# A two-layer hybrid trunk on one NeuronCore: the convolution's first tap on ScalarE into PSUM, wider channel statistics, and the last weight splits placed between taps

## The chip, the core and the metric

The kernel runs on one core of one Trainium2 chip. The metric is the device time of one execution in microseconds; 522.5 us is the median of three runs before the change. The profiled execution is a run of its own, at 522.39 us.

## What is computed

The input x is 512 tokens by 1024 channels in fp32. Layer 0 is attention (two groups of heads, a gate and an output projection). The change lies in layer 1, whose reference, cut to what matters, is

```
val, glu_gate, z = split(rms_norm(x) @ w_in, 3)          # 1024 -> 3 x 1024
u = val * sigmoid(glu_gate)
u = causal depthwise conv(u, conv_w, width 31) + conv_b   # per channel, over tokens
u = silu(layer_norm(u)) * silu(z)                         # layer norm over channels
return x + u @ w_out
```

## The kernel before, in words

Every weight matrix comes in chunks of 256 columns. `fetch` loads a chunk from memory into one of two staging buffers `wst` (L148, on SP's queue); `split_w` (L155) then makes two tensors from it: `hi`, the weight rounded to TensorE's fp32r type, and `lo`, the rest. For most late chunks both come from transfers that POOL issues: a casting transfer `hi<-wst` (L169), and, after ScalarE has written the negated rounded weight into `lo` (L175, or L160 for chunk 32), an accumulating transfer that adds `wst` to it (L179, L161). `ahead(n)` (L807) splits chunks up to n-1 and, behind each, asks for the next chunk's load. That load has to wait until the accumulating transfer out of the same staging buffer has landed. Each product is three matmuls: hi by hi, hi by lo, lo by hi.

In layer 1 the channels are eight tiles of 128. For a tile, TensorE makes value and gate (`glu`, L733), ScalarE a tanh, and VectorE the product `u` (L745, one of three buffers). The 31 taps of the convolution are shared out (`conv_steps`, L748): VectorE adds 15 to 21 of them into `acc`, a PSUM bank (tags `s`, two banks); the first goes into an SBUF tile `first` with the bias added (L763), the second reads `first` and writes `acc`, the rest run in place (L766). ScalarE multiplies the others into `tm` (L775, six buffers; the first of them straight into `pacc`, L772), and POOL adds each `tm` to the SBUF sum `pacc` (L776, two buffers). A tile ends when VectorE adds `acc` and `pacc` (L783, the final sum). `conv_out` (L793) then has TensorE transpose the tile back to tokens (L796), VectorE take statistics of each 128 tokens by 128 channels out of PSUM (L798), and ScalarE copy it to `ctok` (L799).

Tiles 0 and 1 are worked in two halves of 256 tokens, tiles 2 to 5 whole, and tiles 6 and 7, the late ones, in two halves again. Up to L968 the compiler's scheduler sets the order on each engine, by a simulated timeline and program order as priority: the first halves of tiles 6 and 7 (written 6a and 7a here; 18 additions on POOL), and between them `z_chunk` for chunks 28 to 30 with `ahead(34)`, `ahead(35)` and `ahead(36)`, which split chunks 33, 34 and 35 (L966 to L968).

From L1013 the order on TensorE, VectorE, ScalarE and POOL is written out by hand. `na()` emits the next few ScalarE-and-POOL taps of 6b and 7b, the second halves, by the list `AQ` (4, 0, 7, 1, 0, 1, 2, ...), and `nd()` the next few VectorE taps by `DQ` (3, 5, 2, 0, 0, ...). The stretch opens with

```
conv_out(6); z matmuls of tile 6; na(): 4 taps; nd(): 3 taps
conv_out(7); na(): none; z_act(6); norm_stats(0)
z matmuls of tile 7, 6 of 8 steps; na(): 7 taps; nd(): 5 taps
norm_cols(0, 0); ng_t(0, 0); ng_t(0, 1); the other 2 steps of tile 7; norm_cols(0, 1)
```

where `norm_stats` (L900) is two aggregates and an addition on VectorE and a power on POOL (L905), `norm_cols` (L907) normalises `ctok` on VectorE (L911), and `ng_t` transposes it on TensorE (L922). The 5 taps of the second `nd()` are, in this order, 6b's fourth, 7b's first, 6b's fifth, 7b's second, 6b's sixth. Four phases p = 0 to 3 follow for the first half of the tokens: per phase two silus (L928), taps, products with z (L933), rounding (L936), the rest (L939), and 24 output matmuls (L361). Chunks 33 and 34 are used in them, 32 and 35 behind them, beside the second half's `conv_out` and norm.

## Time and profile before

| what | value |
|---|---|
| median of 3 runs (lowest to highest) | 522.5 us (522.39 to 523.61) |
| the profiled execution's own time | 522.39 us |
| its span, first to last instruction | 520.6 us |
| TensorE matmul busy | 503.7 us, 97% of the span |
| VectorE, ScalarE, POOL busy | 373.0, 329.1, 232.6 us |

Times in the rows are microseconds from the span's start unless marked ns. PE is TensorE, PEld its weight loads, DVE VectorE, ACT ScalarE, POOL GpSimd; SP issues plain loads and stores. A row of the order of instructions gives start, duration, engine, line, operation, output<-inputs, shape and count; the square bracket is the engine's idle time just before it and what ended it. TensorE's rows overlap, as its matmuls are pipelined.

### The profile page before, as it was taken

The numbers are of one execution on the slowest core, as the hardware profiler recorded it, in microseconds if no ns is written. First come the engines' busy times: TensorE is split into PE (matmuls) and PEld (weight loads), VectorE is DVE, ScalarE is ACT, GpSimd is POOL, SyncE is SP. The second block draws the span as 40 slices with busy tenths as digits, with TensorE's granted clock in tenths as the row PEclk, the third lists the DMA queues.
The fourth block names the chain that finished last, engine by engine and source line by source line (L and its number), as shares of the span: only waits on it lengthen the run. The fifth ranks groups of instructions, "written<-read, shape, count | busy, mean of one in ns | idle before, by whom it ended". The sixth has DMA issues, their size and how long they took to land.

```text
span 520.6 us, 9754 instructions
## 1 busy us (share of the span) xinstructions
PE 503.7 (97%) x3694; PEld 459.9 (88%) x3694; DVE 373.0 (72%) x788; ACT 329.1 (63%) x668; POOL 232.6 (45%) x255
## 2 busy tenths in 40 slices
PE   8999999999999999999999999999999999769997
PEld 4999998987889988788789999999999888548997
DVE  7745677676465577596685256999999997868741
ACT  4945678777645775576384735998676765377230
POOL 5264852020422233223101113879988985687200
PEclk9999999999999999999999999999999999989999
DMA  8742222302122242402219668488999799962111
GB/s 293 318 145 81 84 81 83 102 24 83 61 102 94 82 111 99 144 14 108 102 52 395 130 205 242 82 211 286 235 306 259 212 270 305 262 170 105 41 51 42
DMA packets 16566, 79.05 MB, mean 152 GB/s; under 512 B 1988, under 2 KB 4352, under 8 KB 8712
## 3 DMA queue, kind: packets, MB, share of 16 engines
q1 hardware_dynamic: 12632, 51.08, 27.1%
q0 software_dynamic: 3744, 27.26, 22.0%
q8 instruction: 29, 0.48, 0.4%
q10 hardware_dynamic: 144, 0.09, 0.1%
q14 instruction: 17, 0.14, 0.1%
HBM read 50.07 MB, written 2.14 MB: 100 GB/s over the span
## 4 chain that ended last, share of the span: by engine, by line
PE 70%; DMA 8%; POOL 7%; ACT 6%; DVE 4%; issue 3%; SPq 0%; POOLq 0%; ACTq 0%
PE mm L361 29%; POOL pacc L776 6%; PE mm L370 6%; PE mm L371 6%; PE mm L372 6%; DMA wst<-in_w_dram 5%; PE st L361 4%; PE o L603 3%; PE tp L526 3%; PE o L361 2%; PE s L510 2%; PE s L512 2%; DMA wlo<-wst 1%; DMA xt<-in_xt_dram 1%; PE s L361 1%
## 5 line engine op out<-in xcount | busy, mean ns | idle before, releaser
L776 POOL TENSOR_TENSOR pacc<-pacc,tm 128x256 f32<-128x256 f32 (+1 forms) x125 | 120.7, 986 | 15.8 <-ACT tm L775 10.1
L766 DVE SCALAR_TENSOR_TENSOR s<-u,parts,s 128x256 f32<-128x256 f32 (+1 forms) x211 | 108.1, 569 | 0.5
L361 PE MATMUL mm<-wlo,hhi 128*128 128x256 f32 (+1 forms) x352 | 98.7, 287 | 0.8 <-DVE wlo L177 0.5
L361 PE MATMUL mm<-whi,hhi 128*128 128x256 f32 (+1 forms) x352 | 98.4, 287 | 0.0
L361 PE MATMUL mm<-whi,hlo 128*128 128x256 f32 (+1 forms) x352 | 98.3, 286 | 0.0
L775 ACT ACTIVATE tm<-u,parts 128x256 f32<-128x256 f32 (+1 forms) x125 | 66.2, 571 | 14.5 <-POOL pacc L776 14.0
L361 PEld LDWEIGHTS mm<-wlo,hhi 128*128 128x128 f32 x352 | 65.8, 190 | 2.0 <-DVE wlo L177 0.8
L361 PEld LDWEIGHTS mm<-whi,hhi 128*128 128x128 f32 x352 | 65.6, 189 | 0.7 <-issue 0.2
L361 PEld LDWEIGHTS mm<-whi,hlo 128*128 128x128 f32 x352 | 65.9, 190 | 0.2
L177 POOL TENSOR_TENSOR wlo<-wst,whi 128x512 fp32r<-128x512 f32 (+1 forms) x22 | 31.0, 1423 | 57.4 <-ACT whi L173 57.4
L173 ACT ACTIVATE whi<-wst 128x512 fp32r<-128x512 f32 (+2 forms) x77 | 49.4, 707 | 5.9 <-DMA wst<-in_w_dram 2.7
L518 POOL TENSOR_TENSOR cb<-cb,mask 128x128 f32<-128x128 f32 x32 | 15.5, 490 | 80.7 <-DVE nm L522 46.2
L523 ACT ACTIVATE p<-p,nm 128x128 f32<-128x128 f32 (+3 forms) x64 | 35.7, 559 | 24.1 <-DVE nm L522 23.6
L177 DVE TENSOR_TENSOR wlo<-wst,whi 128x512 fp32r<-128x512 f32 (+1 forms) x50 | 39.8, 830 | 9.0 <-PE o L361 7.1
L370 PE MATMUL mm<-nhi,wx 128*128 128x256 f32 (+1 forms) x104 | 33.0, 318 | 0.0
L371 PE MATMUL mm<-nlo,wx 128*128 128x256 f32 (+1 forms) x104 | 32.2, 309 | 0.0
L372 PE MATMUL mm<-nhi,wx 128*128 128x256 f32 (+1 forms) x104 | 31.9, 307 | 0.0
L371 PE MATMUL mm<-nlo,whi 128*128 128x256 f32 (+1 forms) x104 | 31.8, 307 | 0.0
L372 PE MATMUL mm<-nhi,wlo 128*128 128x256 f32 (+1 forms) x104 | 31.7, 306 | 0.0
L370 PE MATMUL mm<-nhi,whi 128*128 128x256 f32 (+1 forms) x104 | 31.7, 307 | 0.0
L526 PE MATMUL tp<-identf,p 128*128 128x128 f32 x160 | 28.4, 275 | 1.1 <-ACT p L523 0.7
L396 POOL TENSOR_TENSOR rq<-vq,mhalf 128x16 f32<-128x16 f32 x8 | 26.2, 3272 | 6.2 <-DVE vq L394 6.1
(292 smaller groups left out, 1436.3 us busy)
## 6 DMA issues: line engine op xcount, KB each, us to landing
wst<-in_w_dram SPq DMA_DIRECT2D x33, 1024.0 KB, 5.0
wx<-wst POOLq DMA_DIRECT2D x13, 1024.0 KB, 7.2
wlo<-wst POOLq DMA_DIRECT2D x8, 1024.0 KB, 8.4
whi<-wst POOLq DMA_DIRECT2D x3, 1024.0 KB, 4.5
wst<-in_w_dram SPq DMA_DIRECT2D x2, 1040.0 KB
xs<-in_x_dram SPq DMA_DIRECT2D x4, 512.0 KB, 10.3
cb<-cdram SPq DMA_DIRECT2D x8, 256.0 KB, 3.5
x<-in_x_dram SPq DMA_DIRECT2D x4, 512.0 KB, 6.5
```

The source lines that it names most:

```text
L173: A.activation(hi[:, ks], st[:, ks], AF.Copy)
L177: (V if eng is G and parts == 4 and k % 4 and V0 else eng).tensor_tensor(lo[:, ks], st[:, ks], hi[:, ks].bitcast(F32), op=ALU.subtract)
L361: T.matmul(po, a[:, k, ts], b[:, k, :n], start=first and i == 0, stop=last and i == len(prods) - 1)
L370: T.matmul(po, whi[:, k, cs], a, start=k == 0, stop=False)
L371: T.matmul(po, whi[:, k, cs], b, start=False, stop=False)
L372: T.matmul(po, wlo[:, k, cs], a, start=False, stop=k == KC - 1)
L396: G.tensor_tensor(r, v, mhalf[:, :16].rearrange("p (t h) -> p t h", t=NT), op=ALU.pow)
L523: A.activation(p[:, :w], p[:, :w], AF.Exp, bias=nm, scale=-1.0, accum_out=sm[:, h, t:t + 1])
L526: T.transpose(tp[:, j * P:(j + 1) * P], p[:, j * P:(j + 1) * P], identf)
L766: V.scalar_tensor_tensor(acc[:, o], v, w, first[0][:, :n] if i == 1 else acc[:, o], op0=ALU.mult, op1=ALU.add)
L775: A.activation(tm[:, :n], v, AF.Copy, scale=w)
L776: G.tensor_tensor(pacc[:, o], pacc[:, o], tm[:, :n], op=ALU.add)
```

## The change

The first VectorE tap of a tile becomes a ScalarE activation that writes the PSUM accumulator directly. Statistics of tiles 0 to 3 and of tiles 4 and 5 are taken from `ctok` in SBUF, 512 and 256 channels wide, once the last of them is copied; tiles 6 and 7 keep theirs from PSUM. `pacc` gets a third buffer. The casting transfers of chunks 22, 26, 27, 28, 30, 31, 33, 34 and 35 read the weights in memory and not the staging buffer. The splits of chunks 33 and 34 are ordered behind the ScalarE and the POOL instruction of the 9th and the 17th of the 20 taps of 6a and 7a; the split of chunk 35 moves to the end of phase p = 1. The silu results take pairs out of the buffers of tag `sg`.

```diff
     def split_w(w, ring, eng, parts, cast):
-        st, n = w
+        (st, n), src = w
...
         if cast:
-            G.dma_start(hi, st)
+            G.dma_start(hi.rearrange("p k n -> p (k n)"), w_ap(*src, 0, KC))
...
-    stats = l1.tile([P, NT, KC, 6], F32, name="stats")
+    stats = l1.tile([P, NT, 4, 6], F32, name="stats")
...
             if i == 0:
-                first.append(l1.tile([P, S], F32, tag="first", name="first", bufs=FB))
-                V.tensor_scalar(first[0][:, :n], v, w, cbias[:, ct:ct + 1], op0=ALU.mult,
-                                op1=ALU.add)
+                A.activation(acc[:, o], v, AF.Identity, bias=cbias[:, ct:ct + 1], scale=w)
             else:
-                V.scalar_tensor_tensor(acc[:, o], v, w, first[0][:, :n] if i == 1 else acc[:, o],
-                                       op0=ALU.mult, op1=ALU.add)
+                V.scalar_tensor_tensor(acc[:, o], v, w, acc[:, o], op0=ALU.mult, op1=ALU.add)
...
-        for t in range(t0, t0 + n):
-            V.bn_stats(stats[:, t, ct, :], pt[:, t * P:(t + 1) * P])
+        if ct >= KC - NLATE:
+            for t in range(t0, t0 + n):
+                V.bn_stats(stats[:, t, ct - 4, :], pt[:, t * P:(t + 1) * P])
         A.activation(ctok[:, t0:t0 + n, ct * P:(ct + 1) * P],
                      pt[:, t0 * P:(t0 + n) * P].rearrange("p (t c) -> p t c", t=n), AF.Copy)
+        if ct in (3, 5):
+            for t in range(t0, t0 + n):
+                V.bn_stats(stats[:, t, ct // 5, :], ctok[:, t, 4 * (ct // 5) * P:(ct + 1) * P])
...
-        return l1.tile([P, S], F32, tag="pacc", name="pacc", bufs=2)
+        return l1.tile([P, S], F32, tag="pacc", name="pacc", bufs=3)
...
-        c = cs_[h, k] = l1.tile([P, HT], F32, tag="c", name="c", bufs=CB)
+        if k % 2 == 0:
+            cp[0] = l1.tile([P, 2, HT], F32, tag="sg", name="c", bufs=2)
+        c = cs_[h, k] = cp[0][:, k % 2]
...
+    taps = []
     for i in range(max(len(a6), len(a7) + LAGA)):
         j = i - LAGA
         for f in a6[i:i + 1] + (a7[j:j + 1] if j >= 0 else []):
-            f()
+            taps.append(f())
...
     for c in range(3):
         z_chunk(28 + c, c)
-        ahead(34 + c)
+        if c < 2:
+            with tc.issue_after(taps[TW[c]][0].ins), tc.issue_after(taps[TW[c]][1].ins):
+                ahead(34 + c)
...
             for (c, t), po in zip(units, banks):
                 out1_mm(c, t, po, (2 * p, 2 * p + 1))
+            if p == 1:
+                ahead(36)
```

`TW` is (8, 16), `CB` was 3.

## Rows read from the trace of the kernel before

**Rows 1.** The page's first part: busy time of each engine, its share of the span, and its instructions.

```profile
PE 503.7 (97%) x3694; PEld 459.9 (88%) x3694; DVE 373.0 (72%) x788; ACT 329.1 (63%) x668; POOL 232.6 (45%) x255
```

**Rows 2.** Busy time by stretch: the stretch, its length, then each engine's busy time (instructions), the granted TensorE clock, the DMA share and GB/s.

```profile
320.00:442.50 122.50, 122.07 (x902) 115.43 (x900) 118.72 (x238) 94.00 (x142) 102.64 (x107) 1.00 0.86 239
...
461.20:465.00 3.80, 3.73 (x13) 3.13 (x13) 3.74 (x7) 1.42 (x3) 3.48 (x5) 0.55 0.93 185
478.00:517.80 39.80, 39.25 (x327) 38.48 (x325) 20.78 (x53) 9.89 (x22) 6.85 (x10) 1.00 0.15 51
```

**Rows 3.** The order of TensorE's instructions from 442 us.

```profile
444.35 0.44 PE L796 MATMUL tp<-identf,pacc 128*128 128x128 f32 x2 [1.48 <-DVE pacc L783]
...
452.04 0.41 PE L796 MATMUL tp<-identf,pacc 128*128 128x128 f32 x2 [1.74 <-DVE pacc L783]
...
460.50 0.30 PE L922 MATMUL tp<-identf,ctok 128*128 128x128 f32 x1 [3.92 <-DVE ctok L911]
461.27 1.68 PE L922 MATMUL tp<-identf,ctok 128*128 128x128 f32 x7 [0.47 <-DVE ctok L911]
...
465.53 0.38 PE L361 MATMUL st<-whi,u 128*128 128x256 f32 x1 [0.28 <-ACT u L936]
```

**Rows 4.** The order of VectorE's instructions from 443 us.

```profile
443.87 0.42 DVE L783 TENSOR_TENSOR pacc<-s,pacc 128x256 f32<-128x256 f32 x1 [3.68 <-POOL pacc L776]
...
451.46 0.42 DVE L783 TENSOR_TENSOR pacc<-s,pacc 128x256 f32<-128x256 f32 x1
452.49 0.49 DVE L798 BATCH_NORM_STATS2 stats<-tp 128x6 f32<-128x128 f32 x2 [0.60 <-PE tp L796]
...
453.52 0.17 DVE L904 TENSOR_SCALAR lnv<-mv 128x2 f32<-128x2 f32 x1
...
459.40 3.55 DVE L911 TENSOR_SCALAR ctok<-ctok,mv,lnr 128x512 f32<-128x512 f32 x4 [3.82 <-POOL lnr L905]
```

**Rows 5.** The order of POOL's instructions, the late ones; DMA_DIRECT2D is the issue of a transfer.

```profile
421.08 9.50 POOL L776 TENSOR_TENSOR pacc<-pacc,tm 128x512 f32<-128x512 f32 x9
434.93 0.60 POOL L169 DMA_DIRECT2D whi<-wst  x1 [4.34 <-DMA wst<-in_w_dram]
...
442.43 9.13 POOL L776 TENSOR_TENSOR pacc<-pacc,tm 128x256 f32<-128x256 f32 x12 [0.20 <-ACT pacc L772]
456.02 0.60 POOL L169 DMA_DIRECT2D wx<-wst  x1 [4.47 <-DMA wst<-in_w_dram]
...
458.36 1.01 POOL L905 TENSOR_TENSOR lnr<-lnv,mhalf 128x2 f32<-128x2 f32 x1
```

**Rows 6.** The additions of L776 alone, by stretch: the stretch, its length, POOL's busy time with them (how many), the granted TensorE clock, the DMA share and GB/s.

```profile
430.60:451.60 21.00, 12.04 (x16) 1.00 1.00 298
```

**Rows 7.** The order of ScalarE's instructions from 434 us.

```profile
434.47 1.92 ACT L175 ACTIVATE wlo<-wst 128x2048 fp32r<-128x2048 f32 x1 [5.29 <-DMA wst<-in_w_dram]
...
455.53 1.91 ACT L175 ACTIVATE wx<-wst 128x2048 fp32r<-128x2048 f32 x1 [6.85 <-DMA wst<-in_w_dram]
457.35 0.37 ACT L799 ACTIVATE ctok<-tp 128x256 f32<-128x256 f32 x1
...
458.09 2.89 ACT L775 ACTIVATE tm<-u,parts 128x256 f32<-128x256 f32 x7
```

**Rows 8.** Groups of instructions by line and shape, from 315 us to the end: count, busy us, mean ns of one, and idle time before them.

```profile
L766 DVE SCALAR_TENSOR_TENSOR s<-u,parts,s 128x256 f32<-128x256 f32 x139 | 60.7, 479 | 0.5
L766 DVE SCALAR_TENSOR_TENSOR s<-u,parts,s 128x512 f32<-128x512 f32 x72 | 50.2, 742 | 0.0
L798 DVE BATCH_NORM_STATS2 stats<-tp 128x6 f32<-128x128 f32 x32 | 7.2, 281 | 1.5 <-PE tp L796 1.5
L766 DVE SCALAR_TENSOR_TENSOR s<-u,parts,first 128x256 f32<-128x256 f32 x8 | 5.6, 699 | 0.0
L763 DVE TENSOR_SCALAR first<-u,parts 128x512 f32<-128x512 f32 x4 | 5.1, 1287 | 0.0
L763 DVE TENSOR_SCALAR first<-u,parts 128x256 f32<-128x256 f32 x8 | 4.2, 527 | 0.0
L766 DVE SCALAR_TENSOR_TENSOR s<-u,parts,first 128x512 f32<-128x512 f32 x4 | 4.0, 1010 | 0.0
L775 ACT ACTIVATE tm<-u,parts 128x256 f32<-128x256 f32 x85 | 38.4, 502 | 6.0 <-POOL pacc L776 5.9
L775 ACT ACTIVATE tm<-u,parts 128x512 f32<-128x512 f32 x40 | 27.9, 717 | 8.5 <-POOL pacc L776 8.1
```

**Rows 9.** Pieces of the chain of waits, in order of time: start, length, what.

```profile
413.19 5.05 DMA wst<-in_w_dram
...
426.86 7.53 DMA wst<-in_w_dram
...
444.53 10.91 DMA wst<-in_w_dram
```

**Rows 10.** The order of ScalarE's instructions around the end of phase p = 1.

```profile
468.08 0.90 ACT L775 ACTIVATE tm<-u,parts 128x256 f32<-128x256 f32 x2
469.90 1.02 ACT L928 ACTIVATE c<-tp,parts 128x256 f32<-128x256 f32 x2 [0.92 <-PE tp L922]
```

**Rows 11.** The second half's end of the convolution: the last run of additions on POOL, and the last final sum.

```profile
474.69 10.08 POOL L776 TENSOR_TENSOR pacc<-pacc,tm 128x256 f32<-128x256 f32 x12 [0.32 <-ACT tm L775]
...
484.80 0.42 DVE L783 TENSOR_TENSOR pacc<-s,pacc 128x256 f32<-128x256 f32 x1 [0.29 <-POOL pacc L776]
```

More of the change, by code (lines that the diff above doesn't have):

```diff
@@ L48 @@
 V6 = 3
-FB = 1
 Z6 = 8
 ZK = 6
+TW = (8, 16)
 AQ = (4, 0, 7, 1, 0, 1, 2, 1, 3, 3, 2, 1, 6, 0)
@@ L74 @@
 NLATE = 2
-CB = 3
 LATE1 = 0
@@ L228, in fetch @@
         if i < len(wsrc):
-            raw[i] = load_w(*wsrc[i], 4 if i == 0 else 1)
+            raw[i] = load_w(*wsrc[i], 4 if i == 0 else 1), wsrc[i]
     def split(i):
@@ L755, in tap @@
             return u[:, OFF + i + n0:OFF + i + n0 + n], cw[:, ct, i:i + 1]
-        first = []
         def vstep(i):
@@ L774, in astep @@
             tm = l1.tile([P, S], F32, tag="tm", name="tm", bufs=TMB)
-            A.activation(tm[:, :n], v, AF.Copy, scale=w)
-            G.tensor_tensor(pacc[:, o], pacc[:, o], tm[:, :n], op=ALU.add)
+            return (A.activation(tm[:, :n], v, AF.Copy, scale=w),
+                    G.tensor_tensor(pacc[:, o], pacc[:, o], tm[:, :n], op=ALU.add))
         return ([partial(vstep, i) for i in range(nv)],
@@ L912, in norm_cols @@
                             op0=ALU.subtract, op1=ALU.mult)
-    pts_, cs_ = {}, {}
+    pts_, cs_, cp = {}, {}, [None]
     def ng_t(h, p):
```

## The prediction

> **What bounds the kernel now.** I read the busy table first: TensorE's matmuls fill 97% of the span [rows 1], so only a stretch in which TensorE stands still can give much. The table by stretch shows where. From 320 to 442.5 us TensorE is busy 122.07 of 122.50 us and from 478 to the last matmul 39.25 of 39.80 [rows 2]; nothing that frees another engine there shortens the run by itself. TensorE's order of instructions has the holes: 1.48 us before the transposes of tile 6a, 1.74 before those of 7a, 3.92 and 0.47 before the transposes of the normalised tokens, 7.61 us together [rows 3]. Right behind the longest one the granted clock is 0.55, about the lower level of 1.2 GHz, for 3.8 us [rows 2].
>
> The other engines tell who is late. VectorE's final sum of 6a waited 3.68 us for POOL [rows 4]. POOL had stood 4.34 us in front of the cast of chunk 33 until its load landed, and ScalarE 5.29 us in front of the same chunk's split [rows 5, 7]; additions came to a stop behind both. The first tap of 7a into `pacc` is what POOL waited for again at 442.43 [rows 5]: with two buffers it could not start before tile 5 had been transposed out. Later ScalarE stood 6.85 us for chunk 35's load with tile 7's copy, a silu and seven taps queued behind [rows 7], and POOL 4.47 for the same load with the norm's power behind; VectorE's normalisation waited 3.82 for that power [rows 4, 5].
>
> **The change, part by part.** The sum is made against the profiled execution, 522.39 us, 0.1 below the median of 522.5 (span 520.6, so 1.8 us lie around it). A measurement of this kernel tells differences over about 0.3%, 1.6 us, from no change.
>
> *VectorE.* Without its wait it would have reached the final sum of 7a at 451.46 - 3.68 = 447.8. The change takes off the first taps, 5.1 + 4.2 us less two of 0.53 that belong to the second halves, so 8.2; and the second taps, which read `first`, cost 1.010 where others cost 0.742 (four) and 0.699 against 0.479 (six of the eight), another 2.4 [rows 8]. The statistics of tiles 0 to 5 are 24 instructions of 0.281, 6.7 us; in their place come eight wide ones. No row shows a wide one; nearest are VectorE's taps of 512 and 256 elements, so 4 x 0.742 + 4 x 0.479 = 4.9 and a gain of 1.8, with nothing at the bad end; I take 1. VectorE could thus be through at 447.8 - 11.6 = 436.2. None of it is on TensorE's path; it makes POOL and ScalarE the late ones. Tile 5's wide statistics now stand behind ScalarE's copy, and that copy can stand behind a split: up to the 5.29 us seen, inside the room.
>
> *ScalarE.* Twelve first taps into PSUM. No row has ScalarE write PSUM; its taps into SBUF cost 0.502 and 0.717, so at most about 4 x 0.72 + 8 x 0.50 = 6.9 us, and I take that, since half of it would change nothing: from 320 to 442.5 ScalarE is idle 28 us [rows 2, 8].
>
> *The splits of 33 and 34, casts from memory, third buffer.* At 430.58 POOL had 14 additions of 6a and 7a to go (16 until 451.6 [rows 6], two of them 6b's). I take it that chunk 33's load still lands near 434.4, since it waits for an older transfer, and that ScalarE's split still ends at 434.47 + 1.92 = 436.4 [rows 7]. But the cast no longer waits for that load, so POOL issues it (0.60) and makes the four additions whose products ScalarE has ready, 3.0 us, to 434.2; it waits for the split to 436.4, issues the accumulation (0.87), and does ten more additions, 7.6 us at 0.76, with chunk 34's two issues, 1.5 [rows 5, 6]. Last addition 446.4, final sum of 7a 446.8. Tile 6a's last addition is four before the end and before chunk 34's issues: 446.4 - 3.0 - 1.5 = 441.9, final sum 442.3. The third buffer is what lets 7a's products be there at all.
>
> What could spoil this is the traffic. Chunk 35's load took 10.91 us beside a cast and an accumulation, chunk 32's 5.05 [rows 9]; now the cast of 33, which reads memory, runs during the load of 33 (7.53 before) instead of after it. The price is between nothing and 10.91 - 7.53 = 3.4 us on that load; I take nothing, as the DMA share is already 1.00 there [rows 6] and the bytes are the same, and keep +1.0 on the end (7a 3.4 later is 1.4 past the 2 us in hand below; a part of it is regained). The Trainium skill, DMA: Bandwidth & Descriptors, section "Issuing engines are not separate DMA queues", says that transfers from all issuing engines share the same 16 DMA engines and interleave; by that rule the early cast does slow the load, and the sum below would be -2.8 instead of -3.8. The two loads just quoted agree with it.
>
> *TensorE to the first half's norm.* It is free for 6a at 444.35 - 1.48 = 442.87, and the sum is there: 1.48 gone. The transposes and z of tile 6 take 452.04 - 1.74 - 444.35 = 5.95, so it is at 7a at 448.8 where it was at 452.04, with 2 us in hand: 3.2 gone. The six steps of tile 7 take 460.50 - 3.92 - 452.04 = 4.54, so it is ready for the normalised tokens at 453.4 [rows 3].
>
> Here the change adds a wait. The split of 35 is gone from in front, so the statistics end 0.94 after the transposes as before, and the power could be done at 451.5 [rows 4, 5]. But the five VectorE taps ahead of the normalisation hold 7b's second, and its first now stands on ScalarE behind tile 7's copy, the silu and seven taps, 457.35 to 460.98 = 3.63 us [rows 7]. So: 448.8 + 0.94 + 3.63 + 0.4 for the first tap, then two VectorE taps of 0.4: normalisation at 454.6, not 459.40. Queued behind it are all of TensorE's transposes. The first of them follows 1.1 later, 455.7, so TensorE still stands 2.3 us. From there to the output matmuls the old chain of 6.1 us (459.40 to 465.53 [rows 3, 4]) has the same steps: they start 4.8 earlier. Less idling might keep the clock up, which would shorten the transposes; I count nothing, and -0.4 at best because the silus and products behind them set that chain.
>
> *The split of 35 in phase 1.* ScalarE gets 1.91 us between the taps that end at 468.98 and the silus of phase 2, where it had 0.92 idle waiting for TensorE's transposes [rows 7, 10]: +1.0 on phases 2 and 3, which had no slack. It also moves a cast and an accumulation issue, 0.60 + 0.87, into POOL's phases [rows 5]; the run of twelve additions at the end starts when ScalarE's products come [rows 11], so these lie in POOL's waits. Chunk 35 is used some 15 us later.
>
> *The tail.* The last final sum waited only 0.29 for POOL [rows 11], and both move by the same amount, so behind 478 everything keeps its place relative to TensorE.
>
> Sum: -4.8 + 1.0 = -3.8, so 522.39 - 3.8 = **518.6 us**, with its own range 517 to 520.5. The silus' buffers, four for three, stand at nothing: ScalarE's silus waited for TensorE's transposes, not for a buffer [rows 10].
>
> **The rivals.** *The splits hold as before.* The scheduler had already put the split of 33 behind eight products of 6a and 7a; if the order stays and POOL's accumulation stands right behind the cast, nothing is added in the gap, 7a ends near 451.5 again and TensorE is at its transposes at 452. Then only chunk 35's move counts: normalisation at 452.04 + 0.94 + 3.63 + 0.4 + 0.8 = 457.8 instead of 459.40, and +1.0 in phase 2: 521.8, no change. For it: the 5.29 us are a load's lateness, which the change does not touch. Against: the four products that waited in front of POOL [rows 5].
>
> *No new wait.* If 7b's first tap is no obstacle and the normalisation starts behind the power at 451.5 plus a tap or two, TensorE hardly stands, 7 us come off, and if the split of 35 fits in ScalarE's wait 515.3 is left. Against it is the written-out order.
>
> *VectorE starves behind ScalarE (slower).* In the scheduled part a tile's first tap is in ScalarE's queue among products that wait for POOL, 14 us of such waits in all [rows 8]; it also needs the PSUM bank that the final sum two tiles earlier frees, and that sum waits for POOL. Price: the wait per tile start, six times (tiles 2 to 5, 6a, 7a). VectorE has 448.4 - 436.2 = 12 us in hand, so it decides from 2 us per start; at 3 us 7a comes 6 us late, at 454.8 where it was at 452.04, and the end is 2.8 behind the rival in which the splits hold: 524.6. For it: VectorE was busy 118.72 of 122.50 us [rows 2], so every gap counts. Against: two tiles are in work at once, so a late start is covered by the other's taps.
>
> **How the numbers follow.** Forecast 0.50; no new wait 0.12; the splits hold 0.20; VectorE starves 0.18. Faster is the first two, 0.62; same 0.20; slower 0.18. The range leaves out the slower case and a little at the other end: it reaches from 515.0 (no new wait, or the clock's 0.4 on top) to 523.3 (the splits hold, with the traffic's +1.0 and some).
>
> **What would show it.** Right: no 4.34 and no 6.85 us wait for a load on POOL and ScalarE after 430; TensorE's transposes of 6a without a wait and of 7a near 449; a wait of 2 to 3 us before the first transposes of normalised tokens, with VectorE's last tap released by ScalarE; a new gap of about 1 us before phase 2. Wrong: a hole in TensorE's row before 442; VectorE idle for ScalarE between 350 and 440; a final sum of 7a after 449; or a normalisation released by POOL's power again.

## The result, and the profile after

The changed kernel takes 529.25 us (median of four runs, 529.16 to 529.38) against 522.75 (522.39 to 523.61) for the kernel before: ratio 1.012 with an interval of 1.011 to 1.014. It is slower by 6.5 us where 3.8 less was forecast. The profiled execution took 529.24 us with a span of 527.5, 6.9 more than that of before.

Busy time after, where [rows 1] has before:

```profile
PE 505.8 (96%) x3694; PEld 461.7 (88%) x3694; DVE 363.6 (69%) x760; ACT 333.6 (63%) x680; POOL 229.5 (44%) x255
```

VectorE has 9.4 us less to do and ScalarE 4.5 more. By stretch, with the columns of [rows 2]:

```profile
320.00:442.50 122.50, 122.46 (x905) 115.91 (x903) 109.89 (x208) 98.50 (x155) 104.25 (x113) 1.00 0.83 224
440.00:450.00 10.00, 7.71 (x29) 5.89 (x28) 8.55 (x23) 0.79 (x2) 4.59 (x7) 0.83 1.00 270
450.00:460.00 10.00, 2.57 (x12) 1.77 (x10) 2.26 (x6) 4.71 (x8) 3.03 (x4) 0.80 1.01 314
460.00:470.00 10.00, 8.34 (x30) 6.47 (x31) 6.23 (x15) 4.64 (x12) 5.96 (x8) 0.69 0.18 36
485.70:525.50 39.80, 38.44 (x322) 37.85 (x320) 20.23 (x52) 9.25 (x21) 6.31 (x9) 1.00 0.19 59
```

Up to 442 TensorE is as full as before. From 450 to 460 no engine is busy half the time while the DMA engines move 314 GB/s. The granted clock was at its lower level, 0.50 (1.2 GHz), from 445.8 to 449.0 and from 456 to 466, each time after TensorE had stood; before the change it was so from 461.6 to 464.8 alone. That did not set the end: the steps of tile 7 that ran at it are through at 468, just when the first normalised tokens come. TensorE's order, the rows that answer to [rows 3]:

```profile
445.07 0.41 PE L792 MATMUL tp<-identf,pacc 128*128 128x128 f32 x2 [2.29 <-DVE pacc L779]
461.06 0.66 PE L792 MATMUL tp<-identf,pacc 128*128 128x128 f32 x2 [8.48 <-DVE pacc L779]
...
468.88 0.98 PE L922 MATMUL tp<-identf,ctok 128*128 128x128 f32 x7 [0.47 <-DVE ctok L911]
...
471.83 0.38 PE L360 MATMUL st<-whi,u 128*128 128x256 f32 x1 [0.58 <-ACT u L938]
```

Tile 6a's transposes start 0.7 us later than before, 7a's 9.0 later, the output matmuls 6.3 later (the split of chunk 35 no longer stands between the last two); the other 0.6 of the 6.9 comes behind them. VectorE's order (the rows of [rows 4]) says why 7a is late:

```profile
436.54 3.23 DVE L763 SCALAR_TENSOR_TENSOR s<-u,parts,s 128x256 f32<-128x256 f32 x8 [5.47 <-ACT s L761]
...
444.51 0.41 DVE L779 TENSOR_TENSOR pacc<-s,pacc 128x256 f32<-128x256 f32 x1
...
457.67 2.71 DVE L763 SCALAR_TENSOR_TENSOR s<-u,parts,s 128x256 f32<-128x256 f32 x6 [8.94 <-ACT s L761]
460.49 0.42 DVE L779 TENSOR_TENSOR pacc<-s,pacc 128x256 f32<-128x256 f32 x1
...
466.42 0.88 DVE L763 SCALAR_TENSOR_TENSOR s<-u,parts,s 128x256 f32<-128x256 f32 x2 [2.76 <-ACT s L761]
467.21 2.94 DVE L911 TENSOR_SCALAR ctok<-ctok,mv,lnr 128x512 f32<-128x512 f32 x4
```

Three stands (idle times of the engine), each for a first tap on ScalarE (L761): 5.47 us for 7a's, 8.94 for 6b's, 2.76 for 7b's. The middle one is the costly one. VectorE's queue holds 6b's second tap ahead of 7a's last taps, though the program writes 7a's first: the scheduler laid the written-out stretch over the end of the scheduled one. So 7a cannot end before 6b has begun. From here on load n, cast n and accumulation n are the transfers of chunk n. The chain of waits (start, length, what) goes on from there:

```profile
411.64 11.19 DMA wx<-wst
...
422.89 7.35 DMA wst<-in_w_dram
...
430.26 1.92 ACT lo L159
...
440.03 12.81 DMA wst<-in_w_dram
...
452.93 1.91 ACT wlo L174
...
457.18 0.47 ACT s L761
...
457.67 1.67 DVE s L763 x4
...
460.49 0.43 DVE pacc L779
```

Read it downward: accumulation 30 frees a staging buffer, load 32 follows, then the split of 32 with its accumulation, then load 34, which takes 12.81 us; behind the split of 34 on ScalarE stand a silu, a copy, four products and 6b's first tap, and behind that VectorE. POOL's issues (order of its instructions) show what ran beside load 34:

```profile
411.64 0.93 POOL L178 DMA_DIRECT2D wx<-wst  x1
...
413.50 1.24 POOL L178 DMA_DIRECT2D wx<-wst  x1
...
435.86 0.84 POOL L168 DMA_DIRECT2D whi<-in_w_dram  x1
436.45 1.14 POOL L178 DMA_DIRECT2D wlo<-wst  x1
...
441.89 0.59 POOL L168 DMA_DIRECT2D whi<-in_w_dram  x1
```

The first two are accumulations 30 and 31, 1.9 us apart (12.2 in the run b_p1 below, which has the order of before); casts 33 and 34, now from memory, and accumulation 33 lie on load 34.

### The profile page after: what moved, and what is told of

The parts are those of the page before. It is cut to its first block, busy times and chain, and to the rows that moved or that the text cites. A ratio compares the mean times of both kernels' runs of the same rounds, so it can differ in the third digit from the quotient of the medians.

```text
span 527.5 us, 9718 instructions
## 1 busy us (share of the span) xinstructions
PE 505.8 (96%) x3694; PEld 461.7 (88%) x3694; DVE 363.6 (69%) x760; ACT 333.6 (63%) x680; POOL 229.5 (44%) x255
## 4 chain that ended last, share of the span: by engine, by line
PE 73%; ACT 8%; DMA 8%; DVE 4%; issue 3%; POOL 2%; SPq 0%; POOLq 0%; ACTq 0%; DVEq 0%
PE mm L360 29%; PE mm L370 6%; PE mm L369 6%; PE mm L371 6%; DMA wst<-in_w_dram 5%; PE st L360 4%; PE o L602 3%; PE tp L525 3%; ACT tm L771 3%; DMA wx<-wst 2%; PE o L360 2%; PE s L509 2%; PE s L511 2%; POOL pacc L772 2%; PE st L370 2%
## 5 line engine op out<-in xcount | busy, mean ns | idle before, releaser
L763 DVE SCALAR_TENSOR_TENSOR s<-u,parts,s 128x256 f32<-128x256 f32 (+1 forms) x223 | 116.1, 575 | 21.7 <-ACT s L761 20.0
L772 POOL TENSOR_TENSOR pacc<-pacc,tm 128x256 f32<-128x256 f32 (+1 forms) x125 | 118.9, 1004 | 20.9 <-ACT tm L771 16.4
L771 ACT ACTIVATE tm<-u,parts 128x256 f32<-128x256 f32 (+1 forms) x125 | 64.7, 571 | 4.7 <-POOL pacc L772 4.5
L369 PE MATMUL mm<-nhi,wx 128*128 128x256 f32 (+1 forms) x104 | 33.8, 325 | 0.0
L370 PE MATMUL mm<-nlo,wx 128*128 128x256 f32 (+1 forms) x104 | 33.5, 322 | 0.0
L371 PE MATMUL mm<-nhi,wx 128*128 128x256 f32 (+1 forms) x104 | 33.4, 321 | 0.0
```

The costliest lines, as they stand in the source:

```text
L369: T.matmul(po, whi[:, k, cs], a, start=k == 0, stop=False)
L370: T.matmul(po, whi[:, k, cs], b, start=False, stop=False)
L371: T.matmul(po, wlo[:, k, cs], a, start=False, stop=k == KC - 1)
L763: V.scalar_tensor_tensor(acc[:, o], v, w, acc[:, o], op0=ALU.mult, op1=ALU.add)
L771: return (A.activation(tm[:, :n], v, AF.Copy, scale=w), G.tensor_tensor(pacc[:, o], pacc[:, o], tm[:, :n], op=ALU.add))
L772: G.tensor_tensor(pacc[:, o], pacc[:, o], tm[:, :n], op=ALU.add))
```

## The experiments

Three theories of the lost time stand in the expectations. Theory 1: the casts from memory stretch the loads beside them. Theory 2: the splits of 30 and 31 come close together, and their accumulations make all later loads late. Theory 3, also called the coupling: VectorE's queue stands for first taps that wait on ScalarE behind splits.

Medians of each kernel, and the ratio to the kernel before run on the same chip (its medians lay between 522.3 and 522.7). "After" is the changed kernel, "before + split 35" the kernel before with only the split of chunk 35 moved to phase 1.

| run | kernel | us | ratio, interval |
|---|---|---|---|
| a_first | after, all first taps back on VectorE | 520.9 | 0.995 (0.992 to 0.998) |
| a_late | after, first taps of 6b and 7b back | 523.5 | 1.001 (0.999 to 1.003) |
| a_dq | after, VectorE's list of taps later | 524.9 | 1.003 (1.001 to 1.006) |
| a_cast | after, casts from the staging buffer | 526.9 | 1.007 (1.005 to 1.010) |
| a_dqc | after, both of the last two | 522.3 | 1.000 (0.999 to 1.001) |
| a_place | after, splits placed as before | 526.8 | 1.007 (1.005 to 1.010) |
| a_pacc | after, two partial-sum buffers | 528.4 | 1.010 (1.008 to 1.012) |
| f_cast | a_first, casts from the staging buffer | 522.3 | 1.000 (0.998 to 1.002) |
| b_p1 | before + split 35 | 518.7 | 0.993 (0.991 to 0.996) |
| p_p2 | before, split 35 in phase 2 | 520.9 | 0.999 (0.996 to 1.001) |
| b_first | before, first taps on ScalarE | 524.1 | 1.003 (1.001 to 1.005) |
| p_first | before + split 35, first taps on ScalarE | 522.5 | 1.001 (0.999 to 1.002) |
| b_cast | before, casts from memory | 525.6 | 1.006 (1.004 to 1.009) |
| p_cast | before + split 35, casts from memory | 523.3 | 1.002 (1.000 to 1.004) |
| p_c33 | before + split 35, cast 33 alone from memory | 519.4 | 0.994 (0.992 to 0.996) |
| p_wide | before + split 35, wide statistics | 525.0 | 1.004 (1.003 to 1.006) |
| p_noacc | p_wide without one accumulation | 522.3 | 1.000 (0.999 to 1.002) |
| p_pacc | before + split 35, third buffer | 526.4 | 1.007 (1.004 to 1.009) |

### What holds VectorE: a_first, a_late, a_dq

In a_first and a_late the first tap is VectorE's again, through the SBUF tile, in a_late for 6b and 7b alone:

```diff
-                A.activation(acc[:, o], v, AF.Identity, bias=cbias[:, ct:ct + 1], scale=w)
+                first.append(l1.tile([P, S], F32, tag="first", name="first", bufs=1))
+                V.tensor_scalar(first[0][:, :n], v, w, cbias[:, ct:ct + 1], op0=ALU.mult,
+                                op1=ALU.add)
...
```

> The changed kernel, with all twelve first taps back on VectorE through the SBUF tile; wide statistics, casts from memory, placement and the third buffer stay. TensorE still makes the products of tile 7 in one piece ahead of z chunk 28. Theory 3 (the coupling through ScalarE's queue): both stands of VectorE, 5.47 and 8.94 us, go, VectorE gets 8 us more work, and the time falls to 521 to 524. Theories 1 and 2: load 34 still lands near 452, ScalarE's split with it, and the time stays over 526.

> The changed kernel, with the first taps of 6b and 7b alone back on VectorE; the other ten stay on ScalarE. Theory 3 (the coupling: 7a's last VectorE taps stand behind 6b's second tap, which waits for a first tap queued on ScalarE behind the split of 34): the 8.94 and 2.76 us stands of VectorE go, the final sum of 7a comes near 452 and not 460.5, and the normalisation is then released by ScalarE's copy of tile 7, behind the split that ends at 454.9, near 458 and not 467.2: 520 to 522. Theories 1 and 2 (the late load itself decides, whoever makes the tap, since ScalarE's copies and products wait behind the split all the same): the normalisation stays past 463 and the time over 526.

Both came far nearer to the coupling's answers than to the others': 520.9 where it said 521 to 524, and 523.5, a miss of 1.5 us above its 520 to 522. Load 34 stays late in a_first, and it is no longer in the way of 7a (ScalarE's order):

```profile
453.02 1.92 ACT L174 ACTIVATE wlo<-wst 128x2048 fp32r<-128x2048 f32 x1 [3.73 <-DMA wst<-in_w_dram]
```

Its final sum of 7a starts at 450.71 and the normalisation at 456.88. But its 8.3 us are not the first taps' alone: the scheduler has also put the split of 34 behind tile 6's copy and four products on ScalarE. In a_late the split stands ahead of them as in the changed kernel, and the gain is 5.8. a_dq leaves every load, split and operation alone and moves only VectorE's taps of 6b and 7b, with the two first taps that are in the same list:

```diff
-DQ = (3, 5, 2, 0, 0, 2, 2, 2, 4, 3, 3, 5, 99)
+DQ = (0, 0, 4, 2, 2, 4, 2, 2, 4, 3, 3, 5, 99)
```

> The changed kernel, with only the written-out list of VectorE's taps changed, from (3, 5, 2, 0, 0, 2, 2, 2, ...) to (0, 0, 4, 2, 2, 4, 2, 2, ...): 6b's and 7b's taps start behind the normalisation. TensorE's and POOL's orders, the loads, the splits and the count of instructions stay. Theory 3 (7a's end and the normalisation are late because VectorE's queue holds 6b's second tap ahead of 7a's last taps): the 8.94 and 2.76 us stands go, the final sum of 7a comes near 451 and not 460.5, the normalisation near 458 behind the split of 34 and tile 7's copy, up to 3 us are given back by the taps that now stand in phases 0 and 1: 520 to 524. If the late load of 34 decides whatever the order (copies and products behind it): over 526.

```profile
450.80 0.42 DVE L779 TENSOR_TENSOR pacc<-s,pacc 128x256 f32<-128x256 f32 x1
...
459.40 2.68 DVE L911 TENSOR_SCALAR ctok<-ctok,mv,lnr 128x512 f32<-128x512 f32 x3 [5.69 <-POOL lnr L905]
```

7a ends 9.7 us earlier with the same late load: the stand was one of order. The time falls by 4.4, to 0.9 above the coupling's 520 to 524. What is left is the other half of the same lateness: the norm's power stands on POOL behind accumulation 34 and three additions whose products ScalarE makes behind the split of 34.

### What makes the loads late: a_cast, a_dqc, a_place, a_pacc

a_cast puts back `G.dma_start(hi, st)`; a_dqc has that and a_dq's list.

> The changed kernel, with the casting transfers reading the staging buffer again; everything else of the change stays, and so does the order on TensorE, VectorE and ScalarE. Theory 1 (the casts from memory run beside load 34 and stretch it, 12.6 us where load 34 had taken 5.5 before): load 34 lands 5 to 7 us earlier, the 8.94 us stand of VectorE behind ScalarE's split of 34 shrinks by as much, and the time falls from 529.2 to 523 to 525. Theory 2 (the loads are late because splits 30 and 31 now come together, so that their accumulations land 11 to 15 us after their issue): load 34 is still asked for near 440 and takes over 9 us, and the time stays within 1.5 of 529.2. Theory 3 (VectorE stands because first taps are queued on ScalarE behind a split): the stand stays as long as the split of 34 starts near 453; it says nothing of the load.

> The changed kernel with both cures at once: VectorE's list of taps as in the run that gave 524.9, and the casting transfers reading the staging buffer as in the run that gave 526.9. If the late load of 34 and the order of VectorE's taps are two causes that stand one behind the other (the split of 34, then the copy of tile 7 and the power of the norm), the gains of 4.4 and 2.4 add up: 522 to 523. If the power, which POOL makes behind the accumulation of 34, holds the normalisation wherever the load lands: 524 to 525.5, or later, since POOL then stands for the load in front of the cast as well.

In a_cast the chain has

```profile
439.68 10.85 DMA wst<-in_w_dram
```

so load 34 is 2.0 us shorter and the kernel 2.4 faster: theory 1 explains that much and not the 5 to 7 it claimed. The load is still asked for at 439.7, as theory 2 had it, though the time fell by more than its 1.5. a_dqc takes both gains together (7.0; 4.4 and 2.4 apart): two causes, one behind the other.

```diff
-        if c < 2:
-            with tc.issue_after(taps[TW[c]][0].ins), tc.issue_after(taps[TW[c]][1].ins):
-                ahead(34 + c)
+        ahead(34 + c)                 # a_place
...
-            if p == 1:
-                ahead(36)             # a_place
...
-        return l1.tile([P, S], F32, tag="pacc", name="pacc", bufs=3)
+        return l1.tile([P, S], F32, tag="pacc", name="pacc", bufs=2)    # a_pacc
```

> The changed kernel, with the splits of 33, 34 and 35 placed as before (behind the z chunks, 35 before the hand-written stretch) and no order towards the taps. TensorE's order is the same as in the changed kernel. If the placement makes the loads late: load 34 is asked for before 436 and the time falls under 525. Theories 1 and 2 put the lateness earlier (casts from memory, splits 30 and 31 together), so the loads stay late, and the split of 35, whose load would land near 460, now stands on ScalarE ahead of the normalisation's copy as well: 529 to 533.

> The changed kernel with two partial-sum buffers again; the first taps stay on ScalarE. With two buffers the scheduler puts the splits of 30 and 31 seven rows apart on ScalarE and not two, and that of 32 four rows later and not fourteen. Theory 2 (the loads are late because the accumulations of 30 and 31 share the traffic and are issued late): loads 32, 33 and 34 are asked for 5 us or more earlier, ScalarE's stand for load 34 is under 5 us and not 12.1, and the time is 522 to 525.5. Theory 3 alone: the coupling in VectorE's queue stays, and the time is within 2 of 529.2.

a_place came at 526.8, between its two answers. The split of 34 still starts at 452.98, so the placement is not what makes load 34 late. 7a ends at 453.07, as 6b's first tap now stands ahead of that split, but VectorE then stands 7.83 us for 7b's first tap, which ScalarE makes behind the splits of 34 and 35. In a_pacc the splits of 32 and 34 start 6.0 and 7.9 us earlier, and the time stays at 528.4, within theory 3's answer. Loads in time are not enough there: with two buffers POOL is late instead, as VectorE's waits show (total, times, longest):

```profile
DVE pacc L779 <- POOL pacc L772: 9.7, 3, 5.7
```

### The split of chunk 35 alone: b_p1, p_p2

```diff
-        ahead(34 + c)
+        if c < 2:
+            ahead(34 + c)
...
+            if p == 1:             # 2 in p_p2
+                ahead(36)
```

> The kernel before, with the split of chunk 35 moved to the end of phase p = 1 and nothing else of the change. The prediction's step: no 6.85 us stand of ScalarE and no 4.47 of POOL before the first half's norm, the normalisation released by POOL's power or tile 7's copy near 455 and not 459.4, and about 1.0 given back in phase 2: near 519.5. If the copy of tile 7 or the split's accumulation in phase 1 takes that back: 521 to 523.

518.7 us, faster than the kernel before and the changed one, and the lowest median here. With the first taps still on VectorE the normalisation starts at

```profile
455.39 3.19 DVE L911 TENSOR_SCALAR ctok<-ctok,mv,lnr 128x512 f32<-128x512 f32 x4
```

4.0 us earlier than [rows 4], and the run ends 3.5 earlier by the two profiled executions: the split in phase 1 costs 0.5, not 1.0. The silus of phase 2 start 11.0 us behind the normalisation, where they started 10.5 behind it before.

> The kernel before with the split of chunk 35 moved one phase further, to the end of phase p = 2. The prediction's price for the split in phase 1 was 1.0 us on the phases behind it. If it is that, and the products for POOL's last additions can stand 1.9 us more: 517.5 to 518.7. If ScalarE's products set POOL's last run of additions and so the last final sum: 519 to 521. Chunk 35 is first used some 14 us behind its new place, so its accumulation should land in time.

520.9, within its second answer: not better. Its normalisation starts 1.0 later already, ahead of the moved split, so of the 2.2 us that separate the two only about 1.2 can be the place.

### First taps alone: b_first, p_first

Only the first tap's lines of the change, on each of the two kernels.

> The kernel before, with the twelve first taps on ScalarE into PSUM and nothing else of the change. Theory 3 (the loss is made by VectorE's order standing behind first taps on a ScalarE that stands for weight loads): slower by itself, 525 to 529, with a wait of VectorE for a first tap of several us between 430 and 460. The rival, that the loss needs the late loads of the other parts as well (casts from memory, splits 30 and 31 together): 521 to 523.5, since in the kernel before load 33's 5.29 us on ScalarE was the only long one ahead of 6b's taps.

> The kernel before with the split of 35 in phase 1 (518.7), and with the twelve first taps on ScalarE; casts, loads, buffers and statistics as before. If the first taps cost what they cost without the move (1.5): 519.5 to 521. Theory 3 puts the cost where ScalarE stands for a load ahead of a first tap; with the split of 35 gone from in front of 6b's and 7b's only the forecast's own wait is left, 3.6 us of products ahead of 7b's first tap: 518.5 to 520.5. Above 522 something else in the order pays.

They cost 1.6 and 3.7, so they lose without the late loads of the other parts too. The sizes missed: 524.1 lies between the two answers of b_first, and 522.5 above both ranges of p_first. In b_first VectorE stands 5.00 us for 7a's first tap and 4.20 for 7b's. Its order in p_first:

```profile
439.61 2.06 DVE L762 SCALAR_TENSOR_TENSOR s<-u,parts,s 128x256 f32<-128x256 f32 x5 [4.48 <-ACT s L760]
...
458.79 0.88 DVE L762 SCALAR_TENSOR_TENSOR s<-u,parts,s 128x256 f32<-128x256 f32 x2 [2.56 <-ACT s L760]
459.57 2.94 DVE L906 TENSOR_SCALAR ctok<-ctok,mv,lnr 128x512 f32<-128x512 f32 x4
```

The 4.48 us are 7a's first tap behind the splits of 33 and 34. The 2.56 us are the forecast's own wait, 7b's first tap behind a copy, a silu and seven products. Together with 7a's end, 2.0 later (453.09 against 451.06), it puts the normalisation 4.2 us behind b_p1's.

### Casts from memory alone: b_cast, p_cast, p_c33, f_cast

`G.dma_start(hi..., w_ap(...))` for all nine chunks, for chunk 33 alone (p_c33), or taken back from a_first (f_cast).

> The kernel before, with the nine casting transfers reading memory and nothing else of the change; TensorE's and VectorE's orders are the same. Theory 1 (casts from memory stretch the loads beside them): load 33 or 35 lands 2 to 5 us later than in the kernel before, 524 to 526. The prediction's own reading (POOL no longer stands 4.34 and 4.47 us in front of the casts, the traffic costs nothing): 519 to 522. Nothing in it: within 1 of 522.5.

> The kernel before with the split of 35 in phase 1 (518.7), and with all nine casting transfers reading memory. Theory 1: the loads land 2 to 6 us later as in the run without the move, which cost 3.1: 521 to 524. If the casts cost only by way of chunk 35's split, which the move takes off the path: 518 to 519.5.

> The kernel before with the split of 35 in phase 1 (518.7), and with the casting transfer of chunk 33 alone reading memory. The prediction's step (POOL no longer stands 4.0 us in front of that cast, the products that ScalarE has ready are added in the gap, 6a and 7a end up to 3 us earlier, the bytes are the same and the traffic costs nothing): 516.5 to 518. Theory 1 (the transfer is issued as soon as POOL comes to it, behind accumulation 32, and runs beside accumulations 31 and 32 and in front of load 33, which lands 3 to 6 us later, with ScalarE's split behind it): 519.5 to 523.

> The changed kernel with the first taps on VectorE again (which ran 520.9) and with the casting transfers reading the staging buffer again as well; the orders on TensorE and VectorE are those of that run. If the 2.3 us that the casts from memory cost the changed kernel are the lateness of load 34, which still held ScalarE from 449.2 to 453.0 in that run: 518 to 519.5. If what is left there is set by something else (POOL now waits for the load in front of the cast, and the norm's power stands behind it): 520.5 to 523.

All nine cost 3.1 and 4.6, as theory 1 had it; by run they spread widely (522.7 to 528.9, 520.4 to 524.4). Chunk 33's alone does nothing that can be told (519.4 against b_p1's 518.7 on another chip, ranges that overlap). Its traces show the two sides that cancel. POOL issues the cast behind accumulation 32, 12 us ahead of its old place, and load 33 takes 9.45 us where b_p1's took 6.74:

```profile
422.72 0.86 POOL L170 DMA_DIRECT2D whi<-in_w_dram  x1
...
439.22 0.87 POOL L182 DMA_DIRECT2D wlo<-wst  x1 [5.28 <-ACT wlo L178]
```

```profile
427.48 9.45 DMA wst<-in_w_dram
```

The 4.0 us that POOL no longer stands in front of the cast it stands in front of the accumulation instead. f_cast came within its second answer, 1.4 us slower than a_first, so there the casts from memory seem to gain. POOL's orders, f_cast and then a_first, show that the reason given with that answer is not what holds the norm:

```profile
453.44 0.59 POOL L168 DMA_DIRECT2D whi<-wst  x1 [8.96 <-DMA wst<-in_w_dram]
455.17 0.85 POOL L178 DMA_DIRECT2D wlo<-wst  x1 [1.14 <-ACT wlo L174]
...
458.78 0.72 POOL L910 TENSOR_TENSOR lnr<-lnv,mhalf 128x2 f32<-128x2 f32 x1
```

```profile
455.24 0.86 POOL L178 DMA_DIRECT2D wlo<-wst  x1 [4.30 <-ACT ctok L801]
455.85 1.00 POOL L910 TENSOR_TENSOR lnr<-lnv,mhalf 128x2 f32<-128x2 f32 x1
```

POOL does stand for load 34 in front of the cast, but accumulation 34 is issued at the same time in both. The power is later because three additions stand ahead of it in f_cast: there ScalarE has the split of 34 ahead of tile 6's copy and the products, as in the changed kernel, and in a_first behind them. So the 1.4 us cannot be put down to the casts.

### Where wide statistics and the third buffer lose: p_wide, p_noacc, p_pacc

Their lines of the change on before + split 35 (p_pacc with the silus' pairs, for room).

> The kernel before, with the split of 35 in phase 1 and the wide statistics. The prediction's step (a VectorE gain of 1 to 1.8 us that is not on TensorE's path): 518 to 519.5. If what moves is the order, since the splits of 33 and 34 now stand twelve rows apart on ScalarE and not four, so that 34 stands between tile 7's parts: 519.5 to 523.

> The kernel before with the split of 35 in phase 1 and the wide statistics (525.0), and with the accumulating transfer of chunk 31 left out, so that chunk 31's small part holds only the negated rounded weight. In the run with it, splits 30 and 31 stood 5.7 us apart and not 12.2, that transfer ran from 413.7 to 428.0 beside load 32, and load 32 took 11.7 us where it takes 5 alone. Theory 2 (transfers that run together are what makes the loads late): load 32 lands within 6 us of 417 and its split starts before 424 and not at 428.9, load 33 is asked for 5 us or more earlier, POOL's 8.2 and 6.0 us stands shrink by most of it, and the time falls to 517.5 to 520.5. If the new order on the engines costs by itself, whatever the transfers: 523.5 to 525.5.

> The kernel before, with the split of 35 in phase 1 (518.7 by itself) and the third partial-sum buffer (its room from the silus' pairs). The prediction's step (the third buffer lets 7a's products be made earlier): VectorE's final sum of 6a no longer waits 3.4 us for POOL, TensorE's 1.2 and 1.7 us stands before 6a and 7a shrink: 516.5 to 518. If the scheduler spends the buffer on another order of the splits (31 and 32 four rows apart, 33 and 34 five): 518 to 521.

p_wide gives VectorE less to do and costs 6.2, above both of its answers. Its chain against b_p1's, load 32 in each:

```profile
417.15 11.77 DMA wst<-in_w_dram
```

```profile
413.10 5.11 DMA wst<-in_w_dram
```

With the wide statistics in its timeline the scheduler has all of tile 7's value and gate matmuls on TensorE ahead of z chunk 28, where a unit of it stood between them: the last of them starts at 408.6 and not at 414.0. They free the buffers that splits 30 and 31 write, so the two splits start 5.7 us apart (404.25 and 409.94) and not 12.2. The changed kernel has the same order (to 408.5). Accumulation 31 then lies on load 32. p_noacc leaves it out (its small part of chunk 31 is then not the right one): the split of 32 starts at 422.81 and not 428.94, load 33 is asked for 8.3 us earlier, and the time falls by 2.7, less than half of the 6.2. What is left there, VectorE's order shows:

```profile
445.74 1.41 DVE L804 BATCH_NORM_STATS2 stats<-ctok 128x6 f32<-128x256 f32 x4 [9.10 <-ACT ctok L800]
```

The wide statistics of tile 5 wait for ScalarE's copy, and that stands behind the split of 34. In p_wide as a whole POOL's stands of 8.2 and 6.0 us in front of chunks 32 and 34 hold the final sums. So transfers are part of it, new waits in the order the rest.

p_pacc costs 7.6, above both of its answers, by a third way. TensorE's, ScalarE's and VectorE's orders in its profiled execution (524.4 us):

```profile
421.27 0.80 PE L370 MATMUL st<-nhi,whi 128*128 128x512 f32 x1 [6.48 <-ACT sg L744]
```

```profile
418.31 0.60 ACT L799 ACTIVATE ctok<-tp 128x512 f32<-128x512 f32 x1 [8.54 <-DVE stats L798]
...
420.64 0.58 ACT L744 ACTIVATE sg<-st 128x512 f32<-128x512 f32 x1
```

```profile
405.21 10.30 DVE L763 TENSOR_SCALAR first<-u,parts 128x256 f32<-128x256 f32 x1
```

The new order has a copy ahead of tile 7's tanh, the copy waits for VectorE's statistics, and TensorE, which needs the bank that the tanh reads, stands 6.5 us in a stretch where it had hardly stood [rows 2]. The statistics are late because a single first tap stands ahead of them on VectorE for 10.30 us, where the 128x256 ones of before took 0.53 on average [rows 8]. POOL makes additions and issues transfers without a pause in the trace for as long as it lasts. Two 128x512 first taps beside POOL's additions, 4.16 us in a_first and 4.66 in f_cast, were long too (1.29 on average before); why is not shown by an experiment. In the changed kernel the first taps are ScalarE's, so this loss cannot be one of its own. The silus' pairs were not run without the buffer.

## Why the forecast was wrong, point by point

*VectorE's relief* was right in kind and did not matter. Measured, the taps left on VectorE and the first taps on ScalarE are these groups (as [rows 8]):

```profile
L763 DVE SCALAR_TENSOR_TENSOR s<-u,parts,s 128x256 f32<-128x256 f32 x147 | 65.6, 484 | 20.3 <-ACT s L761 18.9
...
L761 ACT ACTIVATE s<-u,parts 128x256 f32<-128x256 f32 x8 | 4.5, 556 | 3.0 <-DVE u L745 3.0
L761 ACT ACTIVATE s<-u,parts 128x512 f32<-128x512 f32 x4 | 3.1, 770 | 1.1 <-DVE pacc L779 1.1
```

VectorE is busy 9.4 us less over the whole run (11.6 forecast up to 7a's end), and stands 20 us for first taps. *ScalarE's taps* cost 7.6 us, above the 6.9 called the most they could. The error is not that size: the step asked how much ScalarE has to do, where the question was what it stands behind.

*The splits of 33 and 34.* Chunk 33's split ended at 436.1 (436.4 forecast) and POOL's last addition of 7a at 444.8 (446.4): these numbers held. The final sum of 7a, forecast from POOL at 446.8, came at 460.49, because VectorE was the late one. That is the step that failed: "VectorE could thus be through at 447.8 - 11.6 = 436.2" took away its work and did not ask who makes its operands. With the operand's wait in, VectorE was through with 7a's taps only at 460.4; with the order alone changed (a_dq) the sum came at 450.80. The chunk that hurt was 34, whose load the text did not follow: it costed chunk 33's.

*The traffic* was taken as nothing in the sum, with 1.0 kept for the range. The casts from memory cost 2.4 in the changed kernel and 3.1 and 4.6 by themselves, so 1.0 was too small. The argument of equal bytes failed: in these runs what counted was which transfer ran beside which. Load 34 took 12.81 us in the changed kernel and 10.85 in a_cast, load 33 9.45 in p_c33 and 6.74 in b_p1. The Trainium skill, DMA: Bandwidth & Descriptors, section "Issuing engines are not separate DMA queues", says that transfers started by different engines run on the same 16 DMA engines and interleave. The two pairs of loads agree with it.

*The new wait for 7b's first tap* was right: it is there, with 2.76 us of VectorE's idle time and, alone in p_first, 2.56. The same question, asked of 6b's first tap, would have found the 8.94. The wait that was named for tile 5's statistics, up to 5.29 us and inside the room, was 9.10 in p_noacc. *The split of 35*: right in sign; b_p1 shows that it carries the whole gain, 3.8 us, the very sum that was forecast for everything. *The third buffer* was costed as what lets 7a's products be there. Alone it let the scheduler reorder and cost 7.6, by a long first tap on VectorE that the changed kernel does not have; taking it out of the changed kernel gained 0.8. The parts don't add up.

*The rivals.* The slower one, VectorE starving behind ScalarE's first taps, was the mechanism, at 0.18 too low a chance. Its place was wrong: 2 to 3 us at each of six starts, for products that wait for POOL. The trace has 14.4 of the 20.0 us at the starts of 7a and 6b, behind splits that wait for loads or follow one that did, and 2.8 at 7b's. "Against: two tiles are in work at once, so a late start is covered by the other's taps" fails when the order puts the other tile's last taps behind the late one. The splits did not hold as before: 7a's last addition came early, at 444.8, and was of no use. Two of the forecast's own signs of being wrong are there, VectorE idle for ScalarE before 440 (5.47 us) and a final sum of 7a after 449.

Under it lies a premise that no step stated: that the engines' order up to the written-out stretch would stay. The scheduler makes that order from its own timeline of the work, and p_wide shows that a small relief there moves splits and transfers by more than the relief is worth. Open stays how the 10.5 us between b_p1 and the changed kernel divide among its parts, since each costs 3.7 to 7.6 alone and some undo others: the placement that gains 3.8 in b_p1 costs 2.5 in the changed kernel, by a_place, where the order behind taps comes with it. The ordering of the splits of 33 and 34 behind taps was not run by itself, and whether b_p1's order could be held with the wide statistics or the third buffer in it was not tried either.

## What to carry to other kernels

Before moving an operation to a less busy engine, read what stands in front of it in that engine's queue (a load's wait above all), and what stands behind its reader in the reader's queue; the sum of busy times says neither. Where a scheduler sets the order, measure each part of a change alone: a gain of one part (3.8 us here) was hidden under others that lost. A price measured alone need not carry over either, as that of the third buffer did not. In this kernel two staging buffers made a chain of load, split, accumulation and load; with accumulations 30 and 31 close together the next split came late, and leaving one out brought it forward by 6.1 us.

## What the runs showed of the hardware

A load of 1 MB took 5.1 us beside one cast and, in its last 1.2 us, an accumulation (b_p1, load 32), 9.45 beside an accumulation, a cast from memory and the next load (p_c33, load 33), 11.77 beside a cast and an accumulation (p_wide, load 32), and 12.81 beside an accumulation and two casts from memory (after, load 34). ScalarE's first tap into PSUM was dearer than its products into SBUF, 0.556 against 0.503 us for 128x256 and 0.770 against 0.716 for 128x512; it also adds a bias, and no run separates the two. A VectorE first tap of 128x256 took 10.30 us beside POOL's additions and issues (p_pacc), where 0.53 was the mean before. Statistics over a wide row are cheap, below the bounds taken from taps:

```profile
L800 DVE BATCH_NORM_STATS2 stats<-ctok 128x6 f32<-128x512 f32 x4 | 2.5, 681 | 0.0
L795 DVE BATCH_NORM_STATS2 stats<-tp 128x6 f32<-128x128 f32 x8 | 2.0, 288 | 1.1 <-PE tp L792 1.1
L800 DVE BATCH_NORM_STATS2 stats<-ctok 128x6 f32<-128x256 f32 x4 | 1.4, 410 | 0.0
```

512 elements out of SBUF take 0.681 us where four times 128 out of PSUM take 1.15. By count and mean the eight wide ones need 4.4 us of VectorE where 24 narrow ones took 6.7 [rows 8]: a gain of 2.4 where the forecast took 1.
